# Storing one row of 16 partitions ahead of the first tile of a rotary embedding kernel

## The chip, the cores and the metric

The kernel runs on one core of a Trainium2 chip. The metric is device time in microseconds (us). Before the change the median of three runs is 161.16 us (161.14 to 161.43). A core has five instruction streams: TensorE (PE) for matrix products, VectorE (DVE), ScalarE (ACT), GpSimd (POOL) and SyncE (SP). Transfers between device memory and the core's on-chip memory are issued from a stream and are then carried out by 16 transfer (DMA) engines. On-chip memory has 128 partitions; a tile is laid out with one line of data in each.

## The reference

The input `x` is 16 batches x 512 positions x 1024 values in 32-bit floats, read as 16 heads of 64 values. Each head is rotated by its position's tables (`cos`, `sin`, 512 x 32):

```
x1, x2 = x[..., :half_dim], x[..., half_dim:]
out = concatenate([x1 * cos - x2 * sin, x1 * sin + x2 * cos], axis=-1)
```

Input and output are 33.5 MB each. For each value there are two products and one sum, so the kernel is mostly movement of data.

## The kernel before

Two batches form a "run": 1024 positions laid over 128 partitions, 8 consecutive positions ("rows") in each, 4 KB a row. There are 8 runs, so 64 rows `u`, each a step of 128 partitions x 1024 values. A tile is what one load and one store move: the first and the last run are cut into two tiles of 4 rows (16 KB per partition, 2 MB in all), and the other six are one tile of 8 rows (32 KB per partition, 4 MB). That makes 10 tiles. The buffer `x_sb` is a ring of 40 rows, so five runs are in flight; results overwrite the input in the ring, and the store reads them from there.

- ACT (`on_scalar`) issues all loads. The first six tiles are issued at once, with the two tables behind the first. The load of a later run waits at a fixed row for the stores of the run whose place it takes: `ae.wait_ge(sem_out[k], 16 * stores_of(k))` in L186. One transfer adds 16 to its semaphore, and `stores_of(k)` counts the stores of run `k`, two for run 0.
- DVE (`on_vector`) multiplies a row by cos into PSUM (L286) and, for most rows, adds the sine part (L297). Each L297 raises `sem_v`.
- POOL (`on_gpsimd`, L252) multiplies the swapped halves by sin, one or two rows at a time.
- PE (L216) does the addition for 21 of the rows, with an identity matrix, and ACT then copies the sum out of PSUM (L183).
- SP (`on_sync`) issues all stores. For the last row of each tile it waits until all rows up to it are done (`wait_added`, L131) and issues one store of the whole tile (L160). After the last it waits for the remaining stores.

Each stream keeps its own order; there is no planner. Tile 0 is rows 0 to 3 of run 0; all its rows are added by DVE, none by PE. `in_sbuf` and `in_dram` (L111 to L119) give the two sides of a tile's transfer; the store of tile 0 has 128 pieces of 16 KB, one per partition.

Of the kernel before, what the change touches and what calls it, by code (L numbers as in the profile page):

```python
# [6 lines left out]
def bass_split_heads_rope_kernel(  # L7
# [20 lines left out]
    P = 128  # L28
    R1 = seq // P
# [11 lines left out]
    tiles = []  # L41
# [31 lines left out]
    EH = H * HD // BANK  # L73
    LEAD = 1
    LAG = 10

    with ExitStack() as stack:
        x_sb = stack.enter_context(nc.sbuf_tensor([P, RING, H, 2, HALF], fp32))
# [9 lines left out]
        sem_out = [stack.enter_context(nc.semaphore(f"out{k}")) for k in range(EARLY)]  # L88
# [20 lines left out]
        outr = out.rearrange("(c b) (s r) h d -> c (b s) r (h d)", b=2, r=R2)  # L109
        xs = x_sb[:].rearrange("p n h t d -> p n (h t d)")  # L110

        def in_dram(view, t):
            c, r0, n = tiles[t]
            return view[c][:, r0:r0 + n, :].rearrange("p r d -> p (r d)")

        def in_sbuf(t):
            c, r0, n = tiles[t]
            k = (c * R2 + r0) % RING
            return x_sb[:, k:k + n].rearrange("p n h t d -> p (n h t d)")  # L119

        def where(u):
            t, r = rows[u]
            return t, r, u % RING
# [7 lines left out]
        def wait_added(eng, u):  # L131

            if n_pe[u]:
                eng.wait_ge(sem_a, n_pe[u])
            if n_comb[u]:
                eng.wait_ge(sem_v, n_comb[u])
# [9 lines left out]

        def stores_of(k):

            return sum(c == k for c, _, _ in tiles)

        def load(eng, t):
            eng.dma_start(in_sbuf(t), in_dram(xr, t)).then_inc(sem_in[t], 16)  # L152
# [1 line left out]
        def on_sync(sp):  # L154
            for u in range(NU):
                t, r, k = where(u)
                if r == tiles[t][2] - 1:
                    wait_added(sp, u)
                    k = u // R2
                    sp.dma_start(in_dram(outr, t), in_sbuf(t)).then_inc(sem_out[k] if k < EARLY else sem_rest, 16)  # L160
            sp.wait_ge(sem_rest, 16 * sum(stores_of(k) for k in range(EARLY, NU // R2)))

        def on_scalar(ae):
            later = {}
            for t, (c, r0, n) in enumerate(tiles):
                if c * R2 + r0 + n <= RING:
                    load(ae, t)
                else:

                    later.setdefault((c * R2 + r0 - RING) // R2 * R2 + R2 - 1 + LAG, []).append(t)  # L170
                if t == 0:
                    for i, (table, sem) in enumerate(((cos, sem_cos), (sin, sem_sin))):
                        ae.dma_start(stage[:, i, :], table.rearrange("(s r) d -> s (r d)", r=R1)).then_inc(sem, 16)  # L173

            ae.wait_ge(sem_i, 2)
            ae.activation(pick[:], ident[:].rearrange("q (s h) -> q h s", h=2)[:, :, None, :].broadcast_to([P, 2, 2, P // 2]), COPY).then_inc(sem_g, 1)  # L176
            ae.wait_ge(sem_t, 2)
            ae.activation(s_sb[:, :, 0, :].rearrange("p (h r) d -> p h r d", h=2), tab_ps[:, :, 1], COPY, scale=-1.0)  # L178
            ae.activation(s_sb[:, :, 1, :].rearrange("p (h r) d -> p h r d", h=2), tab_ps[:, :, 1], COPY).then_inc(sem_s, 1)  # L179
            for u in range(NU):  # L180
                if PE2[u]:
                    ae.wait_ge(sem_e, n_pe[u])
                    ae.activation(xs[:, u % RING, :], t1_ps[:, u % NT1, :], COPY).then_inc(sem_a, 1)  # L183
                for t in later.get(u, ()):
                    k = tiles[t][0] - RING // R2
                    ae.wait_ge(sem_out[k], 16 * stores_of(k))  # L186
                    load(ae, t)
# [71 lines left out]
        def on_vector(ve):  # L259
# [44 lines left out]
            for u in range(NU + LEAD):  # L304
                if u < NU:
                    mul(u)
                if u >= LEAD and not PE2[u - LEAD]:
                    comb(u - LEAD)

        on_sync(nc.sync)  # L310
        on_scalar(nc.scalar)
        on_gpsimd(nc.gpsimd)
# [35 lines left out]
```

## Time and profile before

| What | Value |
|---|---|
| Median of three runs | 161.16 us |
| The profiled execution, its own time | 161.35 us |
| Its span, first to last instruction | 159.9 us |
| Busy: POOL, DVE, PE, ACT | 131.8, 129.3, 66.7, 23.7 us |
| Moved | 67.25 MB, mean 420 GB/s over the span |
| Load issues | 6 of 4096 KB, 4 of 2048 KB (and two tables of 64 KB) |
| Store issues | 6 of 4096 KB, 4 of 2048 KB |
| Issue to landing, median | loads 33.5 us (4 MB) and 19.9 (2 MB); stores 25.0 and 14.9 |
| First store issued, last store issued | 22.30 us, 150.83 us |

Times inside a profile count from the first instruction of the span. The row marked DMA is the mean busy share of the 16 transfer engines in 40 equal slices, in tenths. In the table of queues, q10 carries what ACT issues and q1 what SP issues; the last column is the time of the queue's packets as a share of the time of all 16 engines. In the view by stretches each line gives the stretch, its length, the busy time of PE, PE's weight load, DVE, ACT and POOL with the number of instructions, the granted clock of PE, the busy share of the transfer engines and GB/s. In the timeline, a name with a small q (SPq, ACTq) is the issue of a transfer and not its movement. Apart from these views the trace keeps a record of each packet on the transfer engines: its queue, size, start and duration. Where a text speaks of packet records, it means these.

### The profile page before, as it was taken

How to read it: one execution, taken by the hardware profiler on the slowest of the kernel's cores; microseconds unless marked ns; L12 is line 12 of the kernel's file. 1: busy time of each engine (PE TensorE's matmuls, PEld its weight loads, DVE VectorE, ACT ScalarE, POOL GpSimd, SP SyncE). 2: the span in 40 equal slices, each digit the busy share in tenths (PEclk: the TensorE clock that was granted, in tenths of full speed). 3: DMA queues.
4: the chain of work that ended last, by engine and by line, in shares of the span. 5: the costliest groups of instructions: out<-in, count | busy, mean ns of one | idle time of the engine just before them, and what ended most of it. 6: DMA issues, size and time to landing. Idle time of an engine off the chain costs nothing.

```text
span 159.9 us, 494 instructions
## 1 busy us (share of the span) xinstructions
PE 66.7 (42%) x94; PEld 22.6 (14%) x94; DVE 129.3 (81%) x115; ACT 23.7 (15%) x25; POOL 131.8 (82%) x41
## 2 busy tenths in 40 slices
PE   6050006338932762286209540098509860880000
PEld 1020002012301220122002110022102220220000
DVE  0009986799999999999799927999999989989700
ACT  0410000202220222020400204002500250031000
POOL 1009999999999999999999999599999999598000
PEclk9999999999995799569965998555985589567555
DMA  5999998999999999999999999999999999999896
GB/s 164 411 441 459 393 508 344 447 406 426 471 406 447 479 393 395 492 418 402 418 492 393 418 492 402 402 475 389 479 397 418 451 418 488 410 402 484 373 438 279
DMA packets 3169, 67.25 MB, mean 420 GB/s; under 512 B 352, under 2 KB 608, under 8 KB 608
## 3 DMA queue, kind: packets, MB, share of 16 engines
q10 hardware_dynamic: 1728, 33.69, 49.8%
q1 hardware_dynamic: 1440, 33.56, 48.7%
q14 instruction: 1, 0.01, 0.0%
HBM read 33.69 MB, written 33.55 MB: 420 GB/s over the span
## 4 chain that ended last, share of the span: by engine, by line
DMA 49%; DVE 16%; POOL 13%; issue 7%; PE 6%; ACT 2%; ACTq 1%; DVEq 0%; SPq 0%
DMA x_sb<-in_x_dram 27%; DMA out_dram<-x_sb 18%; POOL t_sb L252 13%; DVE x_sb L297 8%; DVE t_ps L286 6%; PE t_ps L216 5%; DMA stage<-in_sin_dram 4%; DVE t_sb L279 2%; ACT x_sb L183 1%; PE tab_ps L200 1%; ACTq L152 0%; ACTq L173 0%; ACT s_sb L178 0%; ACT s_sb L179 0%; DVE tab_ps L265 0%
## 5 line engine op out<-in xcount | busy, mean ns | idle before, releaser
L252 POOL TENSOR_TENSOR t_sb<-x_sb,s_sb 128x2048 f32<-128x2048 f32 (+1 forms) x35 | 131.1, 3775 | 14.9 <-ACT s_sb L179 10.3
L216 PE MATMUL t_ps<-t_sb,ident 128*128 128x512 f32 x84 | 61.9, 888 | 70.6 <-DVE t_ps L286 48.8
L286 DVE TENSOR_TENSOR t_ps<-x_sb,tab_ps 128x1024 f32<-128x1024 f32 x64 | 76.7, 1221 | 17.4 <-ACT s_sb L179 10.5
L297 DVE TENSOR_TENSOR x_sb<-t_ps,t_sb 128x1024 f32<-128x1024 f32 x43 | 52.3, 1219 | 3.2 <-POOL t_sb L252 3.1
L183 ACT ACTIVATE x_sb<-t_ps 128x1024 f32<-128x1024 f32 x21 | 21.3, 1024 | 111.6 <-PE t_ps L216 100.2
L216 PEld LDWEIGHTS t_ps<-t_sb,ident 128*128 128x128 f32 x84 | 20.7, 273 | 111.4 <-DVE t_ps L286 78.8
L279 DVE TENSOR_TENSOR t_sb<-x_sb,tab_ps 128x1024 f32<-128x1024 f32 x6 | 7.3, 1215 | 0.0
L200 PE MATMUL tab_ps<-stage,pick 128*128 128x256 f32 x4 | 2.0, 667 | 4.8 <-DMA stage<-in_sin_dram 4.8
L193 PE MATMUL t_ps<-zero 128*128 128x512 bf16 x6 | 2.7, 630 | 1.3 <-DVE zero L260 1.3
L200 PEld LDWEIGHTS tab_ps<-stage,pick 128*128 128x128 f32 x4 | 1.2, 324 | 5.9 <-issue 5.7
L176 ACT ACT_TABLE_LOAD x1 | 1.3, 1283 | 4.8 <-issue 4.8
L193 PEld LDWEIGHTS t_ps<-zero 128*128 128x128 bf16 x6 | 0.7, 138 | 2.3 <-DVE zero L260 1.2
L178 ACT ACTIVATE s_sb<-tab_ps 128x256 f32<-128x256 f32 x1 | 0.4, 384 | 4.4 <-PE tab_ps L200 4.4
L260 DVE MEMSET zero<- 128x256 uint32 x1 | 0.3, 272 | 0.9 <-PEq L330 0.9
L227 POOL MEMSET ident<- 128x128 f32 x1 | 0.2, 205 | 0.3 <-POOLq L330 0.3
L176 ACT ACTIVATE pick<-ident 128x256 f32<-128x256 f32 x1 | 0.4, 430 | 0.0
L179 ACT ACTIVATE s_sb<-tab_ps 128x256 f32<-128x256 f32 x1 | 0.4, 378 | 0.0
L229 POOL TENSOR_SCALAR_AFFINE_SELECT ident<-ident 128x128 f32<-128x128 f32 x1 | 0.3, 294 | 0.1
L330 POOL MEMSET const-float32-0.0<- 128x1 f32 x1 | 0.1, 99 | 0.3 <-issue 0.3
L265 DVE TENSOR_SCALAR tab_ps<-tab_ps 128x32 f32<-128x32 f32 x1 | 0.2, 189 | 0.0
L330 POOL MEMSET const-bfloat16-1.0<- 128x1 bf16 x1 | 0.1, 102 | 0.0
L330 POOL MEMSET const-uint8-127<- 128x1 uint8 x1 | 0.1, 102 | 0.0
(1 smaller groups left out, 0.1 us busy)
## 6 DMA issues: line engine op xcount, KB each, us to landing
x_sb<-in_x_dram ACTq DMA_DIRECT2D x6, 4096.0 KB, 33.5
out_dram<-x_sb SPq DMA_DIRECT2D x6, 4096.0 KB, 25.0
x_sb<-in_x_dram ACTq DMA_DIRECT2D x4, 2048.0 KB, 19.9
out_dram<-x_sb SPq DMA_DIRECT2D x4, 2048.0 KB, 14.9
stage<-in_cos_dram ACTq DMA_DIRECT2D x1, 64.0 KB, 7.3
stage<-in_sin_dram ACTq DMA_DIRECT2D x1, 64.0 KB, 7.0
```

The lines of the kernel that those rows point to most:

```text
L176: ae.activation(pick[:], ident[:].rearrange("q (s h) -> q h s", h=2)[:, :, None, :].broadcast_to([P, 2, 2, P // 2]), COPY).then_inc(sem_g, 1)
L178: ae.activation(s_sb[:, :, 0, :].rearrange("p (h r) d -> p h r d", h=2), tab_ps[:, :, 1], COPY, scale=-1.0)
L179: ae.activation(s_sb[:, :, 1, :].rearrange("p (h r) d -> p h r d", h=2), tab_ps[:, :, 1], COPY).then_inc(sem_s, 1)
L183: ae.activation(xs[:, u % RING, :], t1_ps[:, u % NT1, :], COPY).then_inc(sem_a, 1)
L193: pe.matmul(t1_ps[:, k, b * BANK:(b + 1) * BANK], zero[:, 0:P], zero[:], start=True, stop=True).then_inc(sem_w, 1)
L200: pe.matmul(tab_ps[:, h].rearrange("p c r d -> p (c r d)"), pick[:, h].rearrange("q b s -> q (b s)"), stage[:].rearrange("q c f -> q (c f) ...
L216: ins = pe.matmul(t1_ps[:, u % NT1, b * BANK:(b + 1) * BANK], ident[:], t2[:, b * BANK:(b + 1) * BANK], start=False, stop=True, skip_group ...
L252: pl.tensor_tensor(t2_sb[:, u % NT2:u % NT2 + n], x_sb[:, k:k + n, :, ::-1, :], table[:, :, None, :, :].broadcast_to([P, n, H, 2, HALF]), ...
L279: ve.tensor_tensor(t2_sb[:, u % NT2, :, :, :], swapped(k), over_heads(tab_ps[:, 0, 1, V_ROW - 1:V_ROW + 1, :]), mult)
L286: ve.tensor_tensor(t1_ps[:, u % NT1, :].rearrange("p (h d) -> p h d", d=HALF), x_sb[:, k, :, :, :].rearrange("p h t d -> p (h t) d"), tab_ ...
L297: ve.tensor_tensor(xs[:, k, :], t1_ps[:, u % NT1, :], t2_sb[:, u % NT2, :, :, :].rearrange("p h t d -> p (h t d)"), add,).then_inc(sem_v, 1)
L330: nc = _bacc.Bacc("TRN2", target_bir_lowering=False, num_devices=1)
```

## The change

The store of tile 0 is cut in three. As soon as row 0 is done, SP stores this row of the first 16 partitions: 16 pieces of 4 KB. When row 3 is done, it issues two more transfers: rows 1 to 3 of the same 16 partitions (16 pieces of 12 KB) and all four rows of the other 112 partitions (112 pieces of 16 KB). Together they write the same bytes as before. All three raise the semaphore of run 0, so `stores_of(0)` becomes 4, and the load that takes run 0's place waits for 64 instead of 32. No other tile and no compute instruction is touched.

```diff
+    FIRST = 16
...
-            return sum(c == k for c, _, _ in tiles)
+            return sum(c == k for c, _, _ in tiles) + 2 * (k == 0)
+
+        def rows_dram(p0, p1, r0, r1):
+            return outr[0][p0:p1, r0:r1, :].rearrange("p r d -> p (r d)")
+
+        def rows_sbuf(p0, p1, r0, r1):
+            return x_sb[p0:p1, r0:r1].rearrange("p n h t d -> p (n h t d)")
...
-                if r == tiles[t][2] - 1:
+                if u == 0:
+                    wait_added(sp, u)
+                    sp.dma_start(rows_dram(0, FIRST, 0, 1), rows_sbuf(0, FIRST, 0, 1)).then_inc(sem_out[0], 16)
+                elif u == R1 - 1:
+                    wait_added(sp, u)
+                    sp.dma_start(rows_dram(0, FIRST, 1, R1), rows_sbuf(0, FIRST, 1, R1)).then_inc(sem_out[0], 16)
+                    sp.dma_start(rows_dram(FIRST, P, 0, R1), rows_sbuf(FIRST, P, 0, R1)).then_inc(sem_out[0], 16)
+                elif r == tiles[t][2] - 1:
                     wait_added(sp, u)
                     k = u // R2
                     sp.dma_start(in_dram(outr, t), in_sbuf(t)).then_inc(sem_out[k] if k < EARLY else sem_rest, 16)
```

## The prediction

> **What bounds the kernel now.** I read the page's slices and queue table first, then the rates by stretches, then the moments at which SP issues stores, then the waits.
>
> ```profile
> DMA  5999998999999999999999999999999999999896
> ...
> q10 hardware_dynamic: 1728, 33.69, 49.8%
> q1 hardware_dynamic: 1440, 33.56, 48.7%
> ...
> DMA 49%; DVE 16%; POOL 13%; issue 7%; PE 6%; ACT 2%; ACTq 1%; DVEq 0%; SPq 0%
> ```
>
> These are lines of the page. Queue q10 carries the loads (issued by ACT), q1 the stores (issued by SP). Their packets together fill 49.8 + 48.7 = 98.5% of the 16 transfer engines' time: 157.5 of 159.9 us. No compute engine is above 82%. The chain of waits also names DVE and POOL, but a chain only follows who released whom. The share says more: the transfers hardly ever pause, so the end comes when 67.25 MB have passed.
>
> ```profile
> 0.00:2.00 2.00, 0.75 (x2) 0.28 (x3) 0.27 (x1) 0.00 (x0) 0.70 (x6) 1.00 0.39 74
> 2.00:24.00 22.00, 4.04 (x9) 1.63 (x7) 11.65 (x10) 2.37 (x4) 12.33 (x5) 1.00 1.02 427
> 24.00:36.00 12.00, 4.99 (x6) 1.89 (x7) 9.50 (x10) 1.02 (x1) 12.00 (x4) 1.00 0.96 396
> 36.00:136.00 100.00, 50.20 (x71) 16.49 (x70) 93.59 (x83) 18.22 (x18) 97.38 (x25) 0.78 1.01 434
> 136.00:150.00 14.00, 6.74 (x8) 2.35 (x8) 13.52 (x13) 2.05 (x2) 9.37 (x4) 0.62 0.97 417
> 150.00:158.00 8.00, 0.00 (x0) 0.00 (x0) 0.76 (x1) 0.00 (x0) 0.00 (x0) 0.50 1.00 430
> 158.00:160.00 2.00, 0.00 (x0) 0.00 (x0) 0.00 (x0) 0.00 (x0) 0.00 (x0) 0.50 0.31 131
> ```
>
> The rates by stretches: the last two columns are the transfer engines' busy share and GB/s. A packet is booked where it starts, so shares go slightly over 1. After the head the rate is 434 GB/s over 100 us, and it is the same with loads alone (427 from 2 to 24 us), both, or stores alone (430 from 150 us). One stretch is slower: 396 from 24 to 36 us, exactly where the first store runs. The lost share is small at both ends: about 1.2 us in the first 2 us, 1.4 us in the last 2.
>
> ```profile
> 14.12 1.23 DVE L297 TENSOR_TENSOR x_sb<-t_ps,t_sb 128x1024 f32<-128x1024 f32 x1
> ...
> 22.30 0.38 SPq L160 DMA_DIRECT2D out_dram<-x_sb  x1
> 33.67 0.34 SPq L160 DMA_DIRECT2D out_dram<-x_sb  x1
> ...
> 144.50 0.33 SPq L160 DMA_DIRECT2D out_dram<-x_sb  x1
> 150.83 0.33 SPq L160 DMA_DIRECT2D out_dram<-x_sb  x1
> ```
>
> The timeline: row 0 is finished at 14.12 + 1.23 = 15.35 us, the first store is issued at 22.30, the last at 150.83. The last transfer of 2 MB needs 2.10 MB / 434 GB/s = 4.8 us, but lands 9.1 us after its issue (159.9). So at 150.83 some 4 us of older stores were still ahead of it: compute leads the transfers by that much, less about 1 us from an issue to its first packet (the first load: issued at 0.80, first packet record at 1.81). Compute could be some 3 us later without moving the end.
>
> ```profile
> ACT x_sb L183 <- DMA out_dram<-x_sb: 11.4, 2, 7.2
> ```
>
> From the waits: ACT stands 11.4 us for stores before it issues the loads that reuse the ring. That is no pause of the load queue: the load issued at 56.31 us starts only after the one ahead, whose last packet record is at 69.8.
>
> **The change part by part.** The sum is made against the profiled execution: 159.9 us of span and 1.4 us around it, 161.35. It is 0.19 us above the median of the three runs, 161.16.
>
> *Earlier issue of row 0.* SP now stops for row 0's DVE add and issues at about 15.4 us. Behind that wait in SP's queue stands only the wait for row 3, due at 22.3: nothing is delayed. The bytes come forward by 7 us, into a stretch already at 427 GB/s; loads move back by 64 KB / 434 GB/s = 0.15 us. Bytes are the same, so 0. It is hidden by compute's 3 us of lead; without it, 0.15 us.
>
> *Two more issues.* One stands at 15.4 us in an idle SP. At 22.3 the 112-partition store is issued one issue later, +0.33 to 0.38 us, while loads keep the engines full: 0. Without that cover, 0.38 us. ACT's wait for this run now counts 4 transfers, 64 instead of 32; its last, the second tile's store issued at 33.67, is unchanged. The 11 us backlog of loads covers a small shift.
>
> *More pieces.* The tile's 128 pieces of 16 KB become 112 of 16 KB, 16 of 12 KB and 16 of 4 KB. In the packet records a 16 KB piece takes 0.611 us and a 32 KB piece 1.213, so one cut costs 2 x 0.611 - 1.213 = 0.009 us, and a semaphore packet 0.009. Each engine gets one more piece and two more semaphore packets: 0.03 us, all on the path.
>
> *A transfer of 16 partitions.* Every transfer in the trace spans 128 partitions, so its rate is not shown. 64 + 192 KB = 0.262 MB at 434 GB/s is 0.60 us. If nothing is lost the cost is 0. If rate goes with the partitions touched, it is an eighth, 54 GB/s: 4.83 us, +4.2. A gain is bounded by the next part. I have no row nearer to either end, so I take the geometric middle, 434 / sqrt 8 = 153 GB/s: 1.71 us, **+1.1 us**. This is on the path: every engine has the same bytes to do and never catches up. [...]
>
> *What the first store does to the loads.* From 24 to 36 us the rate is 396, not 434: 12 x (1 - 396/434) = 1.05 us at most. The packet records say less: load pieces of 32 KB took up to 1.55 us instead of 1.213 from 24.87 us until 36.2, 0.46 us on the mean engine. The change may take this away (0 to -1.05), or lengthen it: the first store's first packet is recorded at 26.26, 4 us after its issue; if an earlier piece removes 3 us of that delay, the slow stretch grows by a quarter, +0.1. I take 0: the slow pieces are all of the one load beside this store, and that load still runs beside its bulk.
>
> Sum: 0.03 + 1.1 = +1.1 us: 162.5 against the profiled execution, **162.3** against the median.
>
> **The rivals.**
>
> *No cost, no gain (no change).* If 16 pieces on 16 engines run at full rate, +0.03 us remains: 161.2. For it: packet records show each engine at its own steady pace, 0.611 us per 16 KB, with loads and stores alternating, so an engine may do load pieces while small store pieces wait. Against: nothing shows engines reading neighbouring partitions at once.
>
> *The store queue's beginning is paid early (faster).* If the slow stretch from 24 us is the price of starting stores at all, 64 KB pay it and not 2 MB: -0.46 us by packet records, 160.7; -1.05 by the stretches, 160.1. It decides if the loads beside the first bulk store run at 1.213 us again. For it: no later store slows its loads. Against: the slow pieces go on for 11 us, not only at the first packet.
>
> *The 112 partitions divide unevenly.* If they go in eights, 14 engines get the 8 pieces they have now and the small pieces on top, 16 KB or 0.61 us: 161.8. If in sevens, 7 x 16 + 16 KB is what each has today, and it costs nothing.
>
> *The bulk store also suffers.* If its 1.84 MB run at half rate, 4.2 us are added: with the small ones 166. For it: its pieces no longer lie over the engines as those of 128 do. Against: it touches seven eighths of the partitions.
>
> **How the numbers follow.** Forecast (small transfers slow, +0.4 to +2.2, so 161.6 to 163.4): 0.35. No cost: 0.28. Faster: 0.22. Uneven: 0.08. Bulk slow: 0.07. A measurement of this kernel tells about 0.2%, 0.32 us, from no change. Slower: 0.35 + 0.08 + 0.07 = 0.50; same 0.28; faster 0.22. The likeliest case is thus just ahead of "no cost", and my time is its time. The range leaves out 0.12 of the faster case below 160.6 and the bulk case above 163.4, about 2 in 10 together; the forecast's own range is 161.6 to 163.4.
>
> **What would show it.** If right, the rate falls between 15 and 20 us and again between 24 and 40 us, by some 0.3 and 0.8 us of transfer time, the rest stays at 434, the last issue still stands 3 us ahead of need, and the last stretch just moves back. If the rate from 24 to 36 us rises to 430, the faster case is right. If all stretches are as before, nothing was at stake. If the final 2 us hold a longer run-out with a low share, the engines are uneven. The forecast is wrong if 16-partition transfers run as fast as the rest, or if the first store's slow stretch hangs on the queue's first use.

## The result, and the profile after

The changed kernel takes 162.45 us (median of six runs, 162.21 to 162.75) against 161.19 us before: a ratio of 1.0069, with a 95% interval of 1.0054 to 1.0085. That is 0.9 to 1.4 us slower. The forecast of 162.3 us and slower held. Its reason held only in part, as the runs below show. The profiled execution has a span of 161.2 us, 1.3 us longer than before.

From the page of the changed kernel, its queues and the two stores issued after row 3 (count, size of each, median us from issue to landing):

```profile
span 161.2 us, 496 instructions
...
q10 hardware_dynamic: 1728, 33.69, 49.3%
q1 hardware_dynamic: 1488, 33.56, 48.6%
...
out_dram<-x_sb SPq DMA_DIRECT2D x1, 1792.0 KB, 20.4
out_dram<-x_sb SPq DMA_DIRECT2D x1, 192.0 KB, 7.0
```

The queues were busy 97.9% of 161.2 us, 157.8 us; before it was 157.5 of 159.9. So the mean transfer engine worked only 0.3 us longer, while the end came 1.3 us later. The view by stretches of the same kernel says where the rest is (columns as in the prediction; the last two are the busy share of the transfer engines and GB/s):

```profile
2.00:24.00 22.00, 4.03 (x9) 1.63 (x7) 11.64 (x10) 2.37 (x4) 12.43 (x5) 1.00 1.00 424
24.00:36.00 12.00, 5.08 (x6) 1.98 (x7) 9.60 (x10) 1.02 (x1) 12.00 (x4) 1.00 0.97 396
36.00:136.00 100.00, 47.84 (x71) 15.74 (x70) 92.50 (x82) 18.22 (x18) 96.23 (x25) 0.80 1.01 433
136.00:150.00 14.00, 6.36 (x8) 2.28 (x8) 13.52 (x13) 2.05 (x2) 10.35 (x4) 0.63 0.97 419
150.00:158.00 8.00, 0.00 (x0) 0.00 (x0) 1.63 (x2) 0.00 (x0) 0.00 (x0) 0.50 0.99 426
158.00:160.00 2.00, 0.00 (x0) 0.00 (x0) 0.00 (x0) 0.00 (x0) 0.00 (x0) 0.50 0.44 188
160.00:162.00 2.00, 0.00 (x0) 0.00 (x0) 0.00 (x0) 0.00 (x0) 0.00 (x0) 0.50 0.02 8
```

From 24 to 36 us the rate is the same 396 GB/s as before, and the other long stretches differ by 3 GB/s or less up to 150 us. What is new is the run-out: a share of 0.44 and then 0.02, where before it was 0.31 and then nothing. A few engines finish long after the others. The semaphore packets of the last store tell when each engine is done. In this table (packet records, one profiled execution each) "mean" and "last" are over the 16 engines:

```
kernel                               mean done   last done   lag
before                                 158.87      159.57    0.69
after                                  159.17      160.83    1.65
after, second profile                  159.03      160.46    1.43
16 + 112, nothing early                159.08      160.17    1.09
16 + 112, nothing early, second        159.27      160.30    1.03
64 + 64                                159.17      159.86    0.70
32 + 96                                159.02      159.64    0.62
row 0 of all 128 early                 158.80      160.58    1.78
```

In the changed kernel the mean engine is 0.30 us later than before and the last one 1.26 us later. Every engine has the same bytes to move (67.25 MB / 16 = 4.20 MB; the linked packets of the last engine come to 4.20), and the engine that fell behind did not catch up: it ended 1.65 us behind the mean. The profile of the kernel with row 0 of all partitions early is of its slowest execution (162.37 us, where the median is 161.71), so its lag is not typical of it.

The packets of the last engine can be linked, since each starts within a few ns of the end of the one before. Its excess over the usual duration is 2.6 us after the change, against 0.8 for the last engine of before. The four largest parts are a 16 KB store piece at 36.1 us (+1.07), the 12 KB piece at 26.3 (+0.50), a store piece at 126.5 (+0.42) and a load piece at 30.3 (+0.28). The first two belong to the new transfers: the 16 KB piece is one of the 112, the 12 KB piece one of the 16.

SP's timeline after the change:

```profile
15.28 0.38 SPq L166 DMA_DIRECT2D out_dram<-x_sb  x1
22.20 0.32 SPq L169 DMA_DIRECT2D out_dram<-x_sb  x1
22.57 0.41 SPq L170 DMA_DIRECT2D out_dram<-x_sb  x1
...
151.70 0.33 SPq L174 DMA_DIRECT2D out_dram<-x_sb  x1
```

The early row is issued at 15.28 us as described; the last store at 151.70 instead of 150.83, still some 2 us before the engines come to it at about 153.7.

### The profile page after: what moved, and what is told of

Read it like the earlier page. It is cut to its first block, busy times and chain, and to the rows that moved or that the text cites. A ratio compares the mean times of both kernels' runs of the same rounds, so it can differ in the third digit from the quotient of the medians.

```text
span 161.2 us, 496 instructions
## 1 busy us (share of the span) xinstructions
PE 64.1 (40%) x94; PEld 21.9 (14%) x94; DVE 129.2 (80%) x115; ACT 23.7 (15%) x25; POOL 131.7 (82%) x41
## 2 busy tenths in 40 slices
DMA packets 3217, 67.25 MB, mean 417 GB/s; under 512 B 384, under 2 KB 640, under 8 KB 656
## 4 chain that ended last, share of the span: by engine, by line
DVE 31%; DMA 23%; issue 15%; PE 11%; POOL 9%; ACT 4%; ACTq 1%; DVEq 0%; SPq 0%
DMA out_dram<-x_sb 19%; DVE x_sb L311 14%; DVE t_ps L300 14%; PE t_ps L230 10%; POOL t_sb L266 9%; DMA stage<-in_sin_dram 4%; ACT x_sb L197 3%; DVE t_sb L293 3%; PE tab_ps L214 1%; ACTq L159 1%; ACTq L187 0%; ACT s_sb L192 0%; ACT s_sb L193 0%; DVE tab_ps L279 0%; DVEq L310 0%
## 5 line engine op out<-in xcount | busy, mean ns | idle before, releaser
L230 PE MATMUL t_ps<-t_sb,ident 128*128 128x512 f32 x84 | 59.3, 852 | 73.8 <-DVE t_ps L300 59.2
L197 ACT ACTIVATE x_sb<-t_ps 128x1024 f32<-128x1024 f32 x21 | 21.3, 1024 | 112.2 <-PE t_ps L230 96.3
L230 PEld LDWEIGHTS t_ps<-t_sb,ident 128*128 128x128 f32 x84 | 20.0, 263 | 113.0 <-DVE t_ps L300 81.2
## 6 DMA issues: line engine op xcount, KB each, us to landing
out_dram<-x_sb SPq DMA_DIRECT2D x3, 2048.0 KB, 11.4
```

The source lines that it names most:

```text
L230: ins = pe.matmul(t1_ps[:, u % NT1, b * BANK:(b + 1) * BANK], ident[:], t2[:, b * BANK:(b + 1) * BANK], start=False, stop=True, skip_group ...
```

## The experiments

Theory N in the texts on record is the forecast's: a transfer of 16 neighbouring partitions is slow. The other letters are explained where they first stand. The diffs are shortened: a line "store rows ..." stands for one transfer. Times compare each kernel with the kernel before on the same chip; where two disagree, the ratio is the better guide.

**The split without the early row, and the early row without the split.**

```diff
# 16 + 112, nothing early
+                if u == R1 - 1:
+                    wait_added(sp, u)
+                    store rows 0 to 3 of partitions 0:16, then of 16:128
# row 0 of all 128 early
+                if u == 0:
+                    wait_added(sp, u); store row 0 of partitions 0:128
+                elif u == R1 - 1:
+                    wait_added(sp, u); store rows 1 to 3 of partitions 0:128
```

> Tile 0 is stored in two transfers, 16 and 112 partitions, both issued after row 3; nothing is issued early. Theory N (16 neighbouring partitions on 16 engines read slowly, some engines fall behind for good, and the last engine sets the end): 162.3 to 162.9 us, as after the change, with some of the 16 pieces well above 0.61 us. Rival E (the early issue itself, by the order of loads and stores, costs the time): 161.2. Rival P (each more transfer or piece costs a fixed price): +0.02, 161.2.

> Row 0 of tile 0 is stored early over all 128 partitions, rows 1 to 3 over all 128 later: early issue without a transfer of 16 partitions. Theory N: 161.1 to 161.4, store pieces at their full rate. Rival E: 162.4 or more, since eight times the bytes come early. Rival P: eight more pieces and one more semaphore packet per engine, 9 x 0.009 = 0.08 us, 161.3. If the slow loads beside the first store are a price of starting the store queue: 160.7.

The split alone took 161.97 us, ratio 1.0048 (1.0025 to 1.0071): most of the loss, without any early issue. That is less than N's 162.3 to 162.9, and more than the 161.2 of both rivals. Its 16 pieces of the small transfer included ones of 0.98, 1.13, 1.53 and 1.63 us where 0.61 is usual. The early row over all partitions took 161.71 us, 1.0022 (1.0004 to 1.004); all its 4 KB pieces took 0.159 us and all its 12 KB pieces 0.460, none slow. So the early row over 128 partitions has no slow piece, yet is a little slower, +0.06 to +0.65 us, which neither N (no loss) nor E (162.4 or more) had said. Its profile, of the slowest of its ten executions, shows the same busy time and one late engine:

```profile
156.00:158.00 2.00, 0.00 (x0) 0.00 (x0) 0.00 (x0) 0.00 (x0) 0.00 (x0) 0.50 0.97 418
158.00:160.00 2.00, 0.00 (x0) 0.00 (x0) 0.00 (x0) 0.00 (x0) 0.00 (x0) 0.50 0.33 139
```

This is the run-out of the kernel with row 0 of all partitions early: 0.33 of the engines' time from 158 us, about as before, although its span is 160.9. One engine alone was busy to 160.6; fifteen were done by 159.3.

**Neighbours or spread, with eight small transfers.**

```diff
+                if u == R1 - 1:
+                    wait_added(sp, u)
# neighbours
+                    for p in range(0, P, 16): store rows 0 to 3 of partitions p:p+16
# spread
+                    for p in range(8): store rows 0 to 3 of partitions p:128:8
```

> Tile 0 is stored after row 3 in eight transfers of 16 neighbouring partitions each. Theory N: the loss of the small transfers eight times over, on the mean engine 8 x 0.17 x 16/12 = 1.8 us and more on the last, 163 to 166. Rival P: seven more semaphore packets per engine, 0.06 us, and the issues of SP hidden: 161.3. Rival E: 161.2.

> As the kernel with eight transfers of 16 neighbouring partitions, but each transfer takes every eighth partition, so that the same number of transfers and pieces of the same size is spread over the 128 partitions. Theory N: most of the loss gone, 161.2 to 161.9. Rival P: the same time as with neighbouring partitions. Rival E: 161.2.

Neighbours: 163.94 us, 1.0155 (1.0119 to 1.0192). Spread: 162.95 us, 1.0102 (1.0083 to 1.0121). With neighbours, 41 of the first 127 store pieces of 16 KB took more than 0.65 us, up to 2.09 us; with spread partitions none of 128 was above 0.614 us. That is what N says of the pieces. But the spread kernel was to come out at 161.2 to 161.9, and it did not: both kernels have further costs that no theory had. The timelines of ACT and SP show one of them, first with neighbours, then spread:

```profile
65.57 0.34 ACTq L161 DMA_DIRECT2D x_sb<-in_x_dram  x1
...
156.15 0.33 SPq L173 DMA_DIRECT2D out_dram<-x_sb  x1
```

```profile
63.32 0.33 ACTq L161 DMA_DIRECT2D x_sb<-in_x_dram  x1
...
154.47 0.33 SPq L173 DMA_DIRECT2D out_dram<-x_sb  x1
```

The load that waits for run 0's stores is issued at 65.57 and 63.32 us instead of 56.31, and ACT, standing in that wait, holds up its copies out of PSUM (17.6 and 18.6 us of waits for stores, 11.4 before); the last store is issued at 156.15 and 154.47 instead of 150.83. These kernels are late in compute as well. It is not the larger cost: by packet records the mean engine of the spread kernel carried packets for 1.1 us longer than before and was without them for 0.6 us longer up to its end; with neighbours it is 1.8 and 1.3 us. In the spread kernel the longer packets are load pieces beside tile 0 (excess from 24 to 48 us 1.0 us on the mean engine, 0.46 before) and six store pieces of 32 KB at about 67 us, 0.85 to 1.21 us slow; why, no run shows. The linked packets show why the stores of tile 0 were late. One engine of the spread kernel did, from 34.57 us: store 16 KB, load 32 KB, store semaphore, load 32 KB, store 16 KB, and so on, two loads to each store. Before, it was one to one: the last engine of that kernel did store 16 KB, load 32 KB, store 16 KB, and so on, from 26.33 to 35.85 us. In both, an engine alternated between its two queues, one packet record at a time, and a semaphore packet, 4 bytes in 0.009 us, was a turn like any other.

**Each transfer alone.** These three leave out part of the store of tile 0.

```diff
# only the 112
+                if u == R1 - 1:
+                    wait_added(sp, u); store rows 0 to 3 of partitions 16:128
# only the 16 neighbours
+                if u == 0:
+                    wait_added(sp, u); store row 0 of partitions 0:16
+                elif u == R1 - 1:
+                    wait_added(sp, u); store rows 1 to 3 of partitions 0:16
# only 16, spread: as above with partitions 0:128:8
```

> The first 16 partitions of tile 0 are not stored at all; the other 112 are stored in one transfer after row 3. 0.262 MB less move, 0.60 us at 434 GB/s. Theory N (only the neighbouring 16 are slow): 160.6, every piece at 0.61 us. Theory M (the 112 partitions also lie badly over the engines, so some of their pieces are slow): 161.0 to 161.6, with pieces near 1.5 us as the changed kernel has two of at 35.6 and 36.1 us.

> As the change, but its transfer of 112 partitions is left out: 16 neighbouring partitions, 4 KB early and 12 KB after row 3. 1.835 MB less move, up to 4.2 us less, fewer if compute sets the end then. Theory N: the 12 KB pieces are slow again, up to some 1.2 us where 0.46 is their pace, and the 4 KB pieces are not. Rival Q (the pieces are slow only because the transfer of 112 is queued behind them): all 12 KB pieces at 0.46 us.

> As the kernel with only the 16 neighbouring partitions, but every eighth partition instead, with the same sizes and moments; 112 partitions are not stored. Theory N: all 12 KB pieces at 0.46 us and the end 0 to 1 us before the one with neighbours. Rival P (small transfers are slow as such): the same slow pieces and the same time.

Only the 112: 161.76 us, 1.0028 (1.0005 to 1.0052), though it moves 0.60 us less. So against its bytes it loses about 1 us by itself, where N said none; that is a little over M's 161.0 to 161.6, and theory M is favoured: the 112 partitions cost time too. How they do it is not shown. Its profiled execution was its fastest, 161.34 us, and has one slow store piece in that stretch, 1.37 us at 35.5, which is 0.05 us on the mean engine. That engine was still 0.5 us later than its bytes say: the rest is mostly load pieces between 72 and 100 us (0.30 us) and store pieces at about 123 us (0.14 us more than before), far from the store of tile 0.

Only the 16: with neighbours 157.38 us, spread 157.64, ratios 0.9752 (0.9721 to 0.9783) and 0.9763 (0.974 to 0.9787), not told apart. In the records, with neighbours ten of the 16 pieces of 12 KB were above 0.460 us, up to 0.707; with spread partitions all 16 took 0.460. Neighbouring partitions are thus shown to slow the pieces, without the 112 behind them (rival Q falls) and not because the transfer is small (rival P falls for the pieces). But it is 0.07 us on the mean engine, and the end does not show it. Neighbouring partitions also write neighbouring rows of the output, and spread ones do not; no run separates the on-chip side from device memory.

These two also settle what the slow load pieces of 24 to 36 us are. Here is the view by stretches, first with neighbours, then spread:

```profile
24.00:36.00 12.00, 5.12 (x6) 2.01 (x7) 9.63 (x10) 1.02 (x1) 12.00 (x4) 1.00 0.98 415
36.00:48.00 12.00, 8.42 (x11) 2.53 (x9) 11.60 (x11) 3.07 (x3) 12.00 (x4) 0.97 0.99 408
```

```profile
24.00:36.00 12.00, 5.10 (x6) 2.01 (x7) 9.62 (x10) 1.02 (x1) 12.00 (x4) 1.00 0.98 421
36.00:48.00 12.00, 6.04 (x11) 1.70 (x10) 12.00 (x11) 3.07 (x3) 12.00 (x4) 0.99 1.00 412
```

Where tile 0 has no bulk store, the slow stretch is not at 24 to 36 us but after 36, beside the store of the second tile. By packet records the excess of the loads there is 0.5 us on the mean engine, as it is beside tile 0's store before. It belongs to the first bulk store, whichever that is; 64 and 192 KB ahead of it do not pay for it.

**Two halves, and 32 with 96.**

```diff
+                if u == R1 - 1:
+                    wait_added(sp, u)
# 64 + 64:  store rows 0 to 3 of partitions 0:64, then of 64:128
# 32 + 96:  store rows 0 to 3 of partitions 0:32, then of 32:128
```

> Tile 0 is stored after row 3 in two transfers of 64 partitions. [...] Rival P: one more semaphore packet per engine, 161.2.

> Tile 0 is stored after row 3 in two transfers, 32 and 96 partitions. Theory M (any transfer whose partitions do not lie over the engines as those of 128 do is slow on some engines): 161.7 to 162.5. Theory N (only the 16 neighbours are slow): 161.2 to 161.5.

The times are 161.64 us, 1.0006 (0.999 to 1.0022), and 161.46 us, 1.0001 (0.9987 to 1.0016): no change in either, or 0.35 us at most. The halves have no slow store piece at all; 32 and 96 have one, 1.30 us at 35.7, and that engine is second last. So neither one transfer more nor a transfer short of 128 partitions costs time that can be told here; theory M in its wide form falls. Both profiles do show a price on the loads: the excess of loads and stores together from 24 to 48 us is 0.84 and 0.79 us on the mean engine, where it is 0.46 before, 0.68 in both profiles of the changed kernel, and 0.48 with row 0 of all partitions early, a cut by rows. With two halves the mean engine is done at 159.17 us, as late as after the change. The run-outs of the two, in the same order:

```profile
158.00:160.00 2.00, 0.00 (x0) 0.00 (x0) 0.00 (x0) 0.00 (x0) 0.00 (x0) 0.50 0.44 188
160.00:162.00 2.00, 0.00 (x0) 0.00 (x0) 0.00 (x0) 0.00 (x0) 0.00 (x0) 0.50 0.00 0
```

```profile
158.00:160.00 2.00, 0.00 (x0) 0.00 (x0) 0.00 (x0) 0.00 (x0) 0.00 (x0) 0.50 0.37 156
160.00:162.00 2.00, 0.00 (x0) 0.00 (x0) 0.00 (x0) 0.00 (x0) 0.00 (x0) 0.53 0.00 0
```

Nothing starts after 160 us. With two halves the share from 158 is 0.44, as after the change, but spread over all engines: the lag of the last is 0.70 us there and 1.65 after the change.

**The early piece alone, and the two main kernels once more.** The first leaves out row 0 of the 112 partitions.

```diff
# early 16, rest over 128
+                if u == 0:
+                    wait_added(sp, u); store row 0 of partitions 0:16
+                elif u == R1 - 1:
+                    wait_added(sp, u); store rows 1 to 3 of partitions 0:128
```

> Row 0 of 16 neighbouring partitions is stored early, then rows 1 to 3 of all 128 partitions; row 0 of the other 112 partitions is not stored. 0.459 MB less move, 1.06 us at 434 GB/s. Theory M (the loss comes with the 112 partitions and the 16 x 12 KB, which this kernel does not have): 160.1 to 160.5. If the early piece of 16 neighbours costs by itself: 160.8 to 161.4.

> The changed kernel once more, for a second profile on the chip of the next three. If slow store pieces of tile 0 (12 KB above 0.46 us, 16 KB near 1.5 us) make the last engine, this profile shows them again and the time is 162.2 to 162.7 us. If the first profile's slow pieces were chance, they lie elsewhere.

> The late split into 16 and 112 partitions once more, beside the changed kernel on one chip, to tell what the early row adds to it. If the split alone is the loss: within 0.3 us of the changed kernel. If the early row has a part: 0.4 us or more below it, as the first comparison with different chips and rounds suggests (161.97 against 162.45).

The early 16 with the rest over 128 took 161.01 us, 0.9965 (0.9952 to 0.9979). By its bytes it should end 1.06 us earlier; it ended 0.34 us earlier by the medians. No store piece of tile 0 was slow, and the mean engine was done at 157.72 us, 1.15 earlier than before, which is what M had said. But the last one was done only at 159.42, a lag of 1.71 us. So it is not the early piece that is slow, and yet the end is near what was expected of that: again a single late engine, and again in a profile of the slowest execution (161.20 us of 160.14 to 161.20).

The changed kernel once more: 162.25 us, 1.0046 (1.0031 to 1.0062). The split without the early row, beside it: 162.00 us, 1.0031 (1.0016 to 1.0045). They are not told apart; the early row's own part lies between nothing and some 0.5 us.

The second profile of the late split shows how much the price of neighbours varies. Here 15 of the 16 pieces of the small transfer were slow, 1.48 us in the mean and up to 2.36 us instead of 0.611: 0.87 us on the mean engine, against 0.18 in its first profile. Thirteen of them began within 0.51 us of each other; in the first profile only eight began within that time of the first piece. The loads beside them lost less, 0.14 us instead of 0.48, and the two executions took nearly the same time, 162.10 and 161.97 us.

The second profile of the changed kernel has its slow pieces in the same places as the first:

```
16 KB store pieces above 0.65 us, start and duration (us), 29 to 41 us
after                          35.65 1.559   36.07 1.685
after, second profile          35.65 1.455   35.87 1.685
16 + 112, nothing early        35.11 1.114   35.28 1.554   35.93 1.433
16 + 112, second               36.51 1.451
only the 112                   35.49 1.371
32 + 96                        35.72 1.302
before; 64 + 64                none
row 0 of all early; early 16, rest over 128: 12 KB pieces, all 0.460
```

In the second profile the last two engines are the two with these pieces, and the last one also had the 12 KB piece (+0.34) and a store piece at 126.0 (+0.52). In the first, one of the two is the last engine. The slow pieces of the small and the large transfer come again and are not chance. The linked packets show the moment: an engine's load of run 2 ends, the load queue's semaphore packet takes its turn, and the engine does two store pieces in a row. The slow piece is the second of the two for all ten pieces of this table (the changed kernel's first: store 0.611 us from 35.45, semaphore, store 1.685 from 36.07). In the kernel before, the linked engines have the same double piece, both at 0.611 us.

## Why the prediction was right or wrong

*What bounds the kernel.* Right: the transfers never pause between 2 and 158 us in either kernel (shares of 0.96 to 1.02 in all stretches), and compute stays ahead. What the prediction passed over is that the end is that of the slowest of 16 engines, 160.83 us after the change, not of the mean, 159.17; it had mentioned uneven engines only as a way to read the last stretch. That reading is what came: the longer run-out with a low share. The sign that the prediction gave for being right did not come: from 15 to 20 us the rate was 431 GB/s against 419 before, and from 24 to 40 us 407 against 406.

*Earlier issue of row 0, two more issues: 0.* Right for the transfers' mean work. Two kernels with an early row have a single engine late by 1.78 and 1.71 us. In both it is the engine that also fetched instructions (last section), and each profile is of the slowest execution of its kernel, so the early row is not shown to be the cause. Between the changed kernel and the late split the difference is 0.25 us by the medians, inside both intervals.

*More pieces: 0.03 us.* Right. 4, 12 and 16 KB pieces take 0.159, 0.460 and 0.611 us at their usual pace, so a cut costs 0.008 us, and there are 32 more semaphore packets.

*A transfer of 16 partitions: +1.1 us on every engine.* This is the step that failed, as a size and in its form. The 4 KB pieces cost nothing. The 12 KB pieces took 0.628 us on the mean engine in one profile and 0.521 in the other instead of 0.460: +0.17 and +0.06 us. Single pieces were up to 0.80 us late. What neighbours do is shown (41 slow pieces of 127 against none of 128 when spread), but as a price of 1.1 us for all engines it did not exist in the changed kernel. Only one profile comes near it: the second of the late split, with 0.87 us for 16 pieces of 16 KB. The geometric middle from which the 1.1 us came rests on no row. The trace does show a low rate for the transfer: the 12 KB pieces ran from 26.18 to 27.67 us, 192 KB in 1.49 us or 132 GB/s. But an engine that was done with its piece went on with loads, so the mean engine lost only 0.17 us. Which engine reads which partition is not in the records, and why neighbours are slow where spread partitions are not was not shown.

*What the first store does to the loads: 0.* Right. Excess of the loads from 24 to 36 us: 0.46 us before, 0.38 and 0.49 after, and the rate is 396 GB/s before and in the first profile, 393 in the second. In other splits these loads did change: the excess is 0.84 us with two halves and 0.14 us in the second profile of the late split. The delay from issue to first packet did not come from the queue's first use: it is 3.5 us for the first small store and 4.0 us for the second.

*The rivals.* No cost: excluded by the interval. Faster: falls, because the slow loads stay with the first bulk store. Uneven division: falls; the transfers give each engine the same share of tile 0, by the linked packets one piece of 4 KB, one of 12 and seven of 16. The bulk store at half rate: false in size, since nearly all of its pieces take 0.611 us, but its cause (its pieces lie otherwise over the engines, the author's guess, which the records do not show) is the nearest to what the last engine shows, a single piece of 1.685 us.

The sum came out right by luck, because two things missed in opposite ways: the small transfers cost the mean engine a sixth of the 1.1 us or less, and the last engine's lag behind the mean grew by 0.96 us in the first profile and 0.74 in the second.

## What to carry to other kernels

Where transfers bind, read the last stretch and the lag of the slowest transfer engine, not only the mean share: here an engine with equal bytes that lost 1.07 us by one piece at 36.1 us did not get it back. Splitting a store by partitions into 16 and 112 did that by slow single pieces, up to 1.685 us; splits of 64 + 64 and 32 + 96 made no change in the time that could be told, though loads and stores from 24 to 48 us lost 0.84 and 0.79 us there on the mean engine, 0.46 before. Each further transfer also cost its queue a turn for its semaphore: with the tile cut into eight, the load that waits for run 0's stores was issued at 65.57 and 63.32 us instead of 56.31.

## What the runs showed of the hardware that was not expected

In these profiles a late engine was often hit again. In the changed kernel the three last engines have store pieces 0.28 to 0.59 us slow between 125.8 and 126.5 us, in the second profile the last two 0.41 and 0.52; engines near the middle have none. In the kernel with row 0 of all partitions early, the engine that fetched 8 KB of instructions at about 61 us lost 0.67 us by that (0.31 for the fetch, 0.36 on the piece behind it) and then 0.42, 0.20 and 0.57 us at 96.3, 121.0 and 126.7, and became the last, 1.8 us behind the mean. It is the same with the early 16 and the rest over 128, and with only 16 spread partitions: the last engine (lags of 1.71 and 1.63 us) is the one with the fetch, and two store pieces on it between 116 and 125 us were 0.22 to 0.55 us slow. All three profiles are of the slowest execution of their kernel. In the kernel before, the engine with that fetch was also the last, by 0.34 us to the next, and had no such late piece. Why an engine out of step meets slow pieces there stays open; no run was made for it. Open as well is why the slow pieces of the 112 partitions come when two store pieces follow each other. None of the versions that store the whole output beats the kernel before.
